# A decoder block in fp32r on one core: the compression's first layer as a stream of its own, a rotary table scaled ahead, more weight tiles, wider splits and another written order

## The chip, the core and the metric

The kernel runs on one core of a Trainium2 chip. A core has five engines with an instruction queue each, worked off in order: TensorE (PE in the profile, PEld for its weight loads), VectorE (DVE), ScalarE (ACT), GpSimd (POOL) and SyncE (SP, which here issues nearly all transfers). They meet at semaphores. The matmuls write to eight PSUM banks of 128 x 512 fp32. The metric is the device time of one execution, in microseconds (us); lower is better.

## The reference

A hybrid decoder block on `x` of 512 tokens by 1024. Cut to what matters:

```python
h = rms_norm(x, norm_pre)
proj = h @ w_in          # split into 15 parts
(q_n, k_c, v_c, k_s, v_s, k_w, v_w, g_n, z_n, q_r, k_r, v_r, z_r, m_a, m_b) = ...
# mixer A: sparse attention, 8 heads of 64, 2 groups
q_n, k_c, k_s, k_w = (apply_rotary(., nsa_ang) for each)
kc = gelu(blocks(k_c) @ cmp_w1_k) @ cmp_w2_k      # compress_blocks: 32 tokens x 64 -> 256 -> 64
vc = gelu(blocks(v_c) @ cmp_w1_v) @ cmp_w2_v
o_a = gated sum of softmax attention over compressed, selected and sliding keys
y_a = (o_a * silu(z_n)) @ w_nsa_o
# mixer B: retention, 4 heads, chunks of 128
q_r = apply_rotary(q_r, ret_ang); k_r = apply_rotary(k_r, ret_ang) * 128 ** -0.5
o_b = retention_sequence(q_r, k_r, v_r)
y_b = (o_b * silu(z_r)) @ w_ret_o
merged = sigmoid(m_a) * y_a + sigmoid(m_b) * y_b
out = x + rms_norm(merged @ w_out, norm_post)
```

Input and output are fp32, and the products are wanted at nearly that precision.

## The kernel before

**Products.** Each fp32 product is three fp32r products: both operands are split into a high part (rounded to fp32r) and a low part (the rest), and high x high, high x low and low x high are summed in PSUM. The transposed input's parts are `hTh` and `hTl`. The weights come as one stream in the order in which they are used. `load_next` issues a transfer of 512 KB on SP into one of four buffers `raw` (L442, L445). `splitter` writes the high half of a raw half-tile into `whi` (ScalarE L224, or VectorE's cast L232), `split_lo` the low half into `wlo` (VectorE's subtraction, L236). A weight tile is one `whi` and one `wlo` of 128 x 512. There are `NW = 9` of them in a ring, and a split waits till the matmuls that read the oldest are through.

**The order is written out.** The kernel is a set of coroutines. `main` goes through the projections and products on TensorE; the others are side work: the tails that read a bank after a block, the attention, the splits. A planner (`Order`) keeps estimated clocks of the engines and asks at each step which coroutine can go on; a table of margins by coroutine (`MARGINS`) and priorities decide among them. What comes out is a fixed sequence for each engine. The hardware only adds the waits.

**The sequence of `main`.** First A (the 512 columns of the sliding and selected keys and values), C (280 columns for the compression and the gates), Q. Then `hidden`, the first layer of the compression, for the keys and then the values: 8 tiles each, 64 matmuls of 256 columns (L272) that read the regrouped tokens `Xs` in `arena_r`. Then the blocks of `PLAN`: Z (the gate of mixer A, 8 tiles with 4 x 3 matmuls of 512 columns each), MA, ZR, QK (queries and keys of the retention), VR (its values), PAIR (QK and ZR of the other two heads), VR of them, MB, NO, RO and so on to the output projection. A block of 128 tokens is 24 matmuls of 512 columns into one bank of the ring `ACC` (banks 84 and 85). Its tail must have read the bank before the next but one block. `hidden` takes one bank of `ACC` for the keys and one for the values. The rings of two banks each besides are `PS` (86, 87) and `PO` (90, 91) for the attention and `PT` (88, 89) for transposes.

**The rotary of the retention.** `tail_qk` runs after each 128-token block of QK, eight times in all: four `scalar_tensor_tensor` of 256 elements that read the bank, multiply by the row's scale `rs` and by a table of sines or cosines (L249), then a subtraction and an addition, then transposes. The table `rtab` has one buffer, loaded again (L1117, on SP) after each step. `ret` is the tail of a value block: high part on ScalarE, low part on VectorE (both scaled by `rs`, into `arena_r`). For the last 128 tokens it first copies the whole bank out and goes on from the copy.

**Sums on POOL.** 25 sums of weights are made in DRAM by transfers that accumulate, issued by `weight_sums`: six after the input's transposed halves are done (flag `hq`), the others after Z's first block.

Of the kernel before, what the change touches and what calls it, by code (L numbers as in the profile page):

```python
# [34 lines left out]
MARGIN = 50  # L35
MARGINS = {'att_cmp': 50.0, 'att_head': 0.0, 'att_out': 1300.0, 'att_sum': 400.0, 'att_unit': 100.0, 'compress': 1300.0, 'ga_split': 1300.0, 'gates': 800.0, 'h_sums': 1000.0, 'keep': 100.0, 'kept': 50.0, 'qk_end': 250.0, 'ret': 20.0, 'ret_state': 0.0, 's_early': 0.0, 's_late': 1000.0, 'seven_end': 0.0, 'split_lo': 20.0, 'splitter': 250.0, 'tail_a': 20.0, 'tail_c': 250.0, 'tail_m': 800.0, 'tail_o': 20.0, 'tail_q': 50.0, 'tail_qk': 600.0, 'tail_yb': 20.0, 'tail_z': 50.0, 'x_split': 0.0, 'zr_end': 1700.0}
SOON = 2
PSOON = 8
# [3 lines left out]
SIGN, SIGN_LAG = 3, 19000.0  # L42
HOLD_C = 300
# [4 lines left out]
DVE_BIAS = 500  # L48


class Order:
# [16 lines left out]
    def spawn(self, gen, prio):  # L68
        self.cos.append([prio, self.n, 0.0, gen])
        self.n += 1  # L70
# [80 lines left out]
def block_kernel(ctx: ExitStack, tc, x, xT, x0s, ws, small, w2s, norm_post, rope_r, dmask, out):  # L151
# [276 lines left out]
    WC = [tuple(at(44, 4480, FR)[:, (2 * p + i) * 280:(2 * p + i + 1) * 280] for i in range(2)) for p in range(KD)]  # L428

    def in_ring(p):  # L430

        return min(p, KD) + max(p - 2 * KD, 0) - sum(min(max(p - 2 * i, 0), 2) for i in sload)
# [24 lines left out]
    def used_up(r):  # L457

        done.append(r)

    nxt = [0]

    def splitter():
        for i, (_, pieces) in enumerate(loads):
            n = sum(pieces)
            for k in range(2):
# [7 lines left out]
                yield lambda: own or in_ring(p) < in_ring(len(done)) + NW  # L474
# [4 lines left out]
                r = max(raws[i][1], done[-1] if done and not own else sfree.get(sload.get(i), 0.0))  # L479
                yield r, "act"  # L480
                m = n // 2
                src = raws[i][0][:, k * m:(k + 1) * m]
                if late >= 0:
                    hi, lo = at(4 * late, 512, FR), at(4 * late + 2, 512, FR)
                elif i in sload:
                    hi, lo = (a[:, k * 512:(k + 1) * 512] for a in SB[sload[i]])
                elif own:
                    hi, lo = WC[p - KD]
                else:
                    hi = wp.tile([P, 512], FR, name="whi", tag="whi", bufs=NW)  # L490
                    lo = wp.tile([P, 512], FR, name="wlo", tag="wlo", bufs=NW)
# [8 lines left out]
                od.spawn(split_lo(p, hi, lo, src, vh, vl, e), rank(p))  # L500
                nxt[0] = p + 1
                yield

    def split_lo(p, hi, lo, src, vh, vl, r):
# [7 lines left out]
        parts.append((hi, lo, r))  # L512
        if p % 2 and len(raws) <= p // 2 + NR:
            load_next()
# [9 lines left out]
    class Block:  # L524


        def __init__(self, nk, n):
            self.base, self.nk, self.n = used[0], nk, n
            used[0] += nk
# [275 lines left out]
    def hidden(i):  # L805

        yield od.need(f"xs{i}")
        yield xr[i] + PE_LAG
        blk = Block(8, 512)
        ph = yield from ACC.get()  # L810
        for c in range(8):
            yield blk.ready(c)
            yield blk.ready(c)
            hi, lo, r = blk.views(c)
            for l in range(2):
                st = Xs[i][:, 2 * c + l].rearrange("p s c -> p (s c)")
                mm(ph[:, 0:256], st, apart(hi[:, l * 256:(l + 1) * 256]), c + l == 0, False, r)
                e = mm(ph[:, 0:256], st, apart(lo[:, l * 256:(l + 1) * 256]), False, c + l == 8)
                yield
            used_up(e)  # L820
        od.spawn(compress(i, ph, e), 1)

    def compress(i, ph, e):
# [4 lines left out]
        e = act(hs, ph[:, 0:256], r=e)  # L828
# [587 lines left out]
    def tail_m(half, i, ps, e):  # L1416
        if half == 0 and i >= 4:
            yield od.need(f"ret0{i - 4}")
# [591 lines left out]
```

## Time and profile before

| | us |
|---|---|
| median of three runs (489.18 to 493.0) | 489.67 |
| the profiled execution | 489.62 |
| its span, first to last instruction | 487.8 |
| TensorE busy | 473.0 (97%) |
| VectorE busy | 422.1 (87%) |
| ScalarE busy | 323.4 (66%) |
| GpSimd busy | 38.9 (8%) |
| DMA, mean over the span | 202 GB/s |

In the lines of the profile, L12 is line 12 of the kernel. A matmul's row has its start, how long it lasted, the tiles it writes and reads, and in brackets how long the engine stood idle ahead of it and what released it. The ends of matmuls are modelled and overlap with the next start, so what a matmul costs is read from start to start.

### The profile page before, as it was taken

The numbers are of one execution on the slowest core, as the hardware profiler recorded it, in microseconds if no ns is written. First come the engines' busy times: TensorE is split into PE (matmuls) and PEld (weight loads), VectorE is DVE, ScalarE is ACT, GpSimd is POOL, SyncE is SP. The second block draws the span as 40 slices with busy tenths as digits, with TensorE's granted clock in tenths as the row PEclk, the third lists the DMA queues.
The fourth block names the chain that finished last, engine by engine and source line by source line (L and its number), as shares of the span: only waits on it lengthen the run. The fifth ranks groups of instructions, "written<-read, shape, count | busy, mean of one in ns | idle before, by whom it ended". The sixth has DMA issues, their size and how long they took to land.

```text
span 487.8 us, 7885 instructions
## 1 busy us (share of the span) xinstructions
PE 473.0 (97%) x2666; PEld 421.2 (86%) x2666; DVE 422.1 (87%) x993; ACT 323.4 (66%) x725; POOL 38.9 (8%) x66
## 2 busy tenths in 40 slices
PE   8999998999999999999999999999999999999993
PEld 7899886889888888887988888998889999988882
DVE  5799899979999999897898999887777868889787
ACT  5796699667789899783686755745435535538542
POOL 3004000112103000000100001010000000000010
PEclk9999999999999999999999999999999999999998
DMA  8989997799987997134678652710574725535914
GB/s 309 394 303 300 321 250 251 190 196 278 318 185 167 345 278 211 59 117 142 134 247 257 225 174 77 204 44 26 164 245 134 254 87 185 188 146 162 310 48 172
DMA packets 31080, 98.75 MB, mean 202 GB/s; under 512 B 3136, under 2 KB 6976, under 8 KB 30272
## 3 DMA queue, kind: packets, MB, share of 16 engines
q1 hardware_dynamic: 24576, 70.85, 43.1%
q0 software_dynamic: 6320, 27.26, 23.2%
q8 instruction: 21, 0.34, 0.3%
q14 instruction: 19, 0.16, 0.1%
q10 hardware_dynamic: 144, 0.14, 0.1%
HBM read 93.52 MB, written 31.98 MB: 257 GB/s over the span
## 4 chain that ended last, share of the span: by engine, by line
PE 82%; ACT 6%; DVE 6%; DMA 3%; issue 2%; SPq 1%; POOLq 0%; POOL 0%; DVEq 0%; ACTq 0%
PE bank L272 70%; PE bank L1251 7%; PE bank L278 4%; ACT whi L224 3%; ACT words L224 2%; DMA raw<-in_stream_dram 2%; DVE wlo L236 2%; DMA words<-in_xT_dram 1%; DVE words L236 1%; DVE words L249 1%; ACT arena_r L224 1%; DVE arena_r L236 1%; ACT rsrow L224 0%; DVE hTl L236 0%; DVE arena_r L249 0%
## 5 line engine op out<-in xcount | busy, mean ns | idle before, releaser
L224 ACT ACTIVATE whi<-raw 128x512 fp32r<-128x512 f32 x176 | 104.6, 623 | 47.7 <-PE bank L272 33.7
L236 DVE TENSOR_TENSOR wlo<-raw,whi 128x512 fp32r<-128x512 f32 x188 | 122.4, 686 | 6.9 <-ACT whi L224 6.5
L272 PE MATMUL bank<-whi,hTh 128*128 128x512 f32 x192 | 72.0, 396 | 3.1 <-DVE arena_r L249 2.2
L272 PE MATMUL bank<-whi,hTl 128*128 128x512 f32 x192 | 68.9, 379 | 0.0
L272 PE MATMUL bank<-wlo,hTh 128*128 128x512 f32 x192 | 68.9, 379 | 0.0
L272 PE MATMUL bank<-arena_r 128*128 128x256 f32 (+2 forms) x328 | 67.5, 328 | 0.0
L224 ACT ACTIVATE arena_r<-bank 128x512 fp32r<-128x512 f32 (+3 forms) x104 | 49.3, 475 | 27.3 <-PE bank L278 26.1
L272 PE MATMUL bank<-arena_r,whi 128*128 128x512 f32 (+1 forms) x208 | 61.5, 371 | 0.0
L236 DVE TENSOR_TENSOR arena_r<-bank,arena_r 128x512 fp32r<-128x512 f32 (+3 forms) x104 | 56.0, 542 | 5.2 <-ACT arena_r L224 4.3
L224 ACT ACTIVATE words<-words,stat 128x384 f32<-128x384 f32 (+3 forms) x112 | 57.2, 542 | 3.2 <-DVE stat L983 2.0
L272 PEld LDWEIGHTS bank<-arena_r 128*128 128x128 f32 x328 | 51.1, 190 | 5.2 <-DVE arena_r L236 0.4
L272 PE MATMUL bank<-hTh,whi 128*128 128x512 f32 (+1 forms) x144 | 51.3, 356 | 0.0
L272 PE MATMUL bank<-hTh,wlo 128*128 128x512 f32 (+1 forms) x144 | 50.2, 348 | 0.3 <-DVE wlo L236 0.3
L272 PE MATMUL bank<-hTl,whi 128*128 128x512 f32 (+1 forms) x144 | 49.9, 347 | 0.0
L272 PEld LDWEIGHTS bank<-whi,hTh 128*128 128x128 f32 x192 | 36.4, 191 | 8.4 <-DVE arena_r L249 2.6
L272 PEld LDWEIGHTS bank<-arena_r,whi 128*128 128x128 f32 x208 | 39.2, 189 | 5.1
L272 PEld LDWEIGHTS bank<-whi,hTl 128*128 128x128 f32 x192 | 36.3, 189 | 5.1
L272 PEld LDWEIGHTS bank<-wlo,hTh 128*128 128x128 f32 x192 | 36.4, 189 | 4.0
L272 PE MATMUL bank<-arena_r,wlo 128*128 128x512 f32 x96 | 36.4, 379 | 0.0
L224 ACT ACTIVATE words<-words 128x512 f32<-128x512 f32 (+3 forms) x47 | 27.4, 583 | 13.5 <-DVE words L236 7.3
L278 PEld LDWEIGHTS bank<-identr,shorts 128*128 128x128 f32 x268 | 30.2, 141 | 6.3 <-ACT words L224 0.5
L278 PE MATMUL bank<-identr,shorts 128*128 128x128 f32 x268 | 31.9, 239 | 0.3 <-DVE words L236 0.3
(182 smaller groups left out, 883.5 us busy)
## 6 DMA issues: line engine op xcount, KB each, us to landing
raw<-in_stream_dram SPq DMA_DIRECT2D x73, 512.0 KB, 4.6
pair<-in_stream_dram POOLq DMA_DIRECT2D x6, 1024.0 KB, 12.1
t<-in_stream_dram POOLq DMA_DIRECT2D x6, 1024.0 KB, 17.4
out<-in_stream_dram POOLq DMA_DIRECT2D x6, 1024.0 KB, 17.0
words<-in_x_dram SPq DMA_DIRECT2D x8, 512.0 KB, 7.9
raw<-s SPq DMA_DIRECT2D x8, 512.0 KB, 4.3
raw<-pair SPq DMA_DIRECT2D x8, 512.0 KB, 4.3
raw<-t SPq DMA_DIRECT2D x8, 512.0 KB, 4.0
```

Of the source, the lines that this page charges most:

```text
L224: S.activation(o, i, func, **kw)
L236: (V if e == "dve" else G).tensor_tensor(o, a, b, op=op)
L249: V.scalar_tensor_tensor(o, a, s, b, op0=op0, op1=op1)
L272: T.matmul(ps, a, b, start=start, stop=stop)
L278: T.transpose(ps, a, idn)
L1251: T.matmul(ps[m], a, apart(b), start=n in first and s + j == 0, stop=n in last and s + j == 5, skip_group_check=True)
```

## The change

It changes these things together:

- `hidden` becomes one coroutine for both halves, started beside Z, and no longer a part of `main`. The weight stream is reordered: Z's weights ahead of the compression's. Both halves share one bank of `PO` (columns 0 to 255 and 256 to 511), taken before Q and given back when the second half is read. The blocks of QK and the tails of MA and MB wait for the flag `hid`.
- The ring of weight tiles becomes a list: nine as before, two more in words 50 to 57 of the shared space for the loads 12 to 19 (Z and the key half of the compression), free after A and the input's halves are done, and four more in the arena for the loads 24 to 31, free once `hidden` is done.
- `rot_table` multiplies the rotary's table by `rs` on ScalarE as soon as it has landed. `tail_qk` then makes two `tensor_tensor` of 512 elements with the table broadcast over the halves, where it made four scaled ones of 256.
- Splits of C's loads, of the loads that the pairs keep and of the last four loads take a whole raw tile at once (1024 or 560 columns).
- `ret` copies out early nowhere (`EARLY_OUT = ()`).
- Other margins, priorities by coroutine (`PRIOS`), other constants of the planner.

The counts of instructions go from 995 to 958 on VectorE and from 652 to 647 on ScalarE. TensorE keeps 2655, SP 170 and POOL 71.

```diff
-MARGIN = 50
-MARGINS = {'att_cmp': 50.0, ...
+MARGIN = 0.0
+MARGINS = {'att_cmp': 0.0, ...
...
+HFIRST, HWANT = 0, 1
+MORE, MORE2 = range(12, 20), range(24, 32)
+EARLY_OUT = ()
...
+    def fits(p):
+        return [(r, i) for r, i in wfree if i < NW or p // 2 in (MORE if i < NW + 2 else MORE2)]
+
+    wtiles.extend((words(50 + 4 * i, 512, FR), words(52 + 4 * i, 512, FR)) for i in range(2))
+    wtiles.extend((at(44 + 4 * i, 512, FR), at(46 + 4 * i, 512, FR)) for i in range(4))
+
+    def more_tiles():
+
+        yield od.need("A0", "A1", "A2", "A3", "hq")
+        wfree.extend((last[1], NW + i) for i in range(2))
+        yield od.need("hid")
+        wfree.extend((hfree[0], NW + 2 + i) for i in range(4))
...
+                wide = i in sload or i >= len(loads) - 4 or KD <= p < 2 * KD
+                if wide and k:
+                    continue
-                yield lambda: own or in_ring(p) < in_ring(len(done)) + NW
+                yield lambda: own or fits(p)
...
-                m = n // 2
+                m = n if wide else n // 2
...
-    def hidden(i):
-
-        yield od.need(f"xs{i}")
-        yield xr[i] + PE_LAG
-        blk = Block(8, 512)
-        ph = yield from ACC.get()
-        for c in range(8):
-            yield blk.ready(c)
-            yield blk.ready(c)
-            hi, lo, r = blk.views(c)
...
+    def hidden(bank):
+
+        for i in range(2):
+            yield od.need(f"xs{i}")
+            yield xr[i] + PE_LAG
+            ph = bank[:, i * 256:(i + 1) * 256]
+            for c in range(8):
+                p = hp[8 * i + c]
+                for _ in range(2):
+                    if HWANT:
+                        wanted[0] = max(wanted[0], p)
+                    yield parts[p][2] + PE_LAG if p < len(parts) else (lambda: p < len(parts))
+                hi, lo, r = parts[p]
+                for l in range(2):
+                    st = Xs[i][:, 2 * c + l].rearrange("p s c -> p (s c)")
+                    mm(ph, st, apart(hi[:, l * 256:(l + 1) * 256]), c + l == 0, False, r)
+                    e = mm(ph, st, apart(lo[:, l * 256:(l + 1) * 256]), False, c + l == 8)
+                    yield
+                used_up(e, p)
+            od.spawn(compress(i, ph, bank, e), 1)
+        hfree[0] = e
+        od.flags.add("hid")
...
+        od.spawn(rot_table(i, od.dma(P * 2048, r)), 1)
+
+    def rot_table(i, e):
+        yield e, "act"
+        rtr[0] = act(rtab, rtab, r=e, scale=rs(i % 4))
+        od.flags.add(f"rt{i}")
...
-        for i in range(2):
-            e = stt(v1[:, :, i, :], pv[:, :, i, :], rs(t), tv[:, 0], OP.mult, OP.mult, e)
-        yield e, "dve"
-        stt(v2[:, :, 0, :], pv[:, :, 1, :], rs(t), tv[:, 1], OP.mult, OP.mult, e)
-        e = stt(v2[:, :, 1, :], pv[:, :, 0, :], rs(t), tv[:, 1], OP.mult, OP.mult, e)
+        e = tt(v1, pv, tv[:, 0].unsqueeze(2).broadcast_to([P, 4, 2, 64]), OP.mult, e)
+        yield e, "dve"
+        e = tt(v2, pv, tv[:, 1].unsqueeze(2).broadcast_to([P, 4, 2, 64]), OP.mult, e)
...
-        if t == NT - 1:
+        if (hp, t) in EARLY_OUT:
...
+        bank = yield from PO.get()
...
-        for i in range(2):
-            yield from hidden(i)
+        od.spawn(hidden(bank), 1)
...
+            if name == "QK":
+                yield od.need("hid")
```

What this does to the order on TensorE is seen first in `hidden`. Before, its matmuls stand in a row, and the value half (bank 85) follows the key half (bank 84):

```order
L272 MATMUL bank0_84<-whi_976,arena_r_83 128x256
L272 MATMUL bank0_84<-wlo_977,arena_r_83 128x256
L272 MATMUL bank0_84<-whi_976,arena_r_83 128x256
L272 MATMUL bank0_84<-wlo_977,arena_r_83 128x256
L272 MATMUL bank1_85<-whi_998,arena_r_83 128x256
L272 MATMUL bank1_85<-wlo_999,arena_r_83 128x256
L272 MATMUL bank1_85<-whi_998,arena_r_83 128x256
L272 MATMUL bank1_85<-wlo_999,arena_r_83 128x256
```

In the changed kernel, at the compression's first tiles, in bank 90; the rows on bank 84 are Z's, those on 86 and 87 the attention's:

```order
L276 MATMUL bank_84<-hTh,whi_167 128x512
L276 MATMUL bank_84<-hTl,whi_167 128x512
L276 MATMUL bank_84<-hTh,wlo_168 128x512
L276 MATMUL bank_90<-whi_173,arena_r 128x256
L276 MATMUL bank_90<-wlo_174,arena_r 128x256
L276 MATMUL bank_90<-whi_173,arena_r 128x256
L276 MATMUL bank_90<-wlo_174,arena_r 128x256
L276 MATMUL bank_90<-whi_175,arena_r 128x256
L276 MATMUL bank_90<-wlo_176,arena_r 128x256
```

One or two tiles of the compression now stand between those of Z.

The second place is the border between VR's first and second block of tokens on TensorE. QK's last block stands in bank 85 ahead of them. Before, bank 84 ends the first block of VR and begins the second, with two matmuls of the attention (bank 91) between:

```order
L272 MATMUL bank_84<-whi,hTh 128x512
L272 MATMUL bank_84<-wlo,hTh 128x512
L272 MATMUL bank_84<-whi,hTl 128x512
L272 MATMUL bank_91<-arena_r 128x512 x2
L272 MATMUL bank_84<-whi,hTh 128x512
L272 MATMUL bank_84<-wlo,hTh 128x512
```

In the changed kernel there:

```order
L276 MATMUL bank_84<-whi_175,hTl 128x512
L276 MATMUL bank_91<-arena_r 128x512 x2
L282 MATMUL bank_88<-identr,shorts_512_1156 128x128
L282 MATMUL bank_88<-identr,shorts_512_1158 128x128
L282 MATMUL bank_88<-identr,shorts_512_1160 128x128
L282 MATMUL bank_88<-identr,shorts_512_1162 128x128
L282 MATMUL bank_89<-identr,shorts_512_1156 128x128
L282 MATMUL bank_89<-identr,shorts_512_1158 128x128
L282 MATMUL bank_89<-identr,shorts_512_1160 128x128
L282 MATMUL bank_89<-identr,shorts_512_1162 128x128
L276 MATMUL bank_85<-whi_173,hTh 128x512
```

Bank 85 follows bank 84, and transposes stand between. At VR's blocks for the other two heads one bank still serves two blocks one after the other in the changed kernel (bank 85 before, bank 84 now).

The third place is ScalarE, at the scaling of the rotary's table (`words_512_136` is `rtab`), a new row among the attention's exponentials and evictions:

```order
L228 ACTIVATE words_256_141<-words_512_127 128x256
L228 ACTIVATE words_512_136<-words_512_136,rs_191 128x512
L228 ACTIVATE arena_r<-bank_88 128x512
L228 ACTIVATE words_512_128<-bank_90 64x512
L228 ACTIVATE arena_r<-bank_89 32x128 x4
```

It stands between two evictions; before, ScalarE had no part in the rotary until its transposes.

More of the change, by code (lines that the diff above doesn't have):

```diff
@@ L427, in block_kernel @@
     raws, parts, done = [], [], []
-    WC = [tuple(at(44, 4480, FR)[:, (2 * p + i) * 280:(2 * p + i + 1) * 280] for i in range(2)) for p in range(KD)]
-    def in_ring(p):
-        return min(p, KD) + max(p - 2 * KD, 0) - sum(min(max(p - 2 * i, 0), 2) for i in sload)
+    WC = [tuple(at(44, 4480, FR)[:, (2 * p + i) * 560:(2 * p + i + 1) * 560] for i in range(2)) for p in range(KD // 2)]
+    wtiles = [tuple(wp.tile([P, 512], FR, name=f"{n}{i}") for n in ("whi", "wlo")) for i in range(NW)]
+    wfree, slot_of = [(0.0, i) for i in range(NW)], {}
+    def fits(p):
[7 more added lines that the diff above has]
+        wfree.extend((hfree[0], NW + 2 + i) for i in range(4))
+    hfree = [0.0]
     hook = {}
@@ L478, in splitter @@
                         load_next()
-                r = max(raws[i][1], done[-1] if done and not own else sfree.get(sload.get(i), 0.0))
+                r = max(raws[i][1], min(fits(p))[0] if not own else sfree.get(sload.get(i), 0.0))
                 yield r, "act"
-                m = n // 2
+                m = n if wide else n // 2
                 src = raws[i][0][:, k * m:(k + 1) * m]
                 if late >= 0:
-                    hi, lo = at(4 * late, 512, FR), at(4 * late + 2, 512, FR)
+                    hi, lo = at(4 * late, 1024, FR), at(4 * late + 4, 1024, FR)
                 elif i in sload:
-                    hi, lo = (a[:, k * 512:(k + 1) * 512] for a in SB[sload[i]])
+                    hi, lo = SB[sload[i]]
                 elif own:
-                    hi, lo = WC[p - KD]
+                    hi, lo = WC[(p - KD) // 2]
                 else:
-                    hi = wp.tile([P, 512], FR, name="whi", tag="whi", bufs=NW)
-                    lo = wp.tile([P, 512], FR, name="wlo", tag="wlo", bufs=NW)
+                    slot = min(fits(p))
+                    wfree.remove(slot)
+                    slot_of[p] = slot[1]
+                    hi, lo = wtiles[slot[1]]
                 vh, vl = hi[:, :m], lo[:, :m]
@@ L511, in split_lo @@
         yield lambda: len(parts) == p
-        parts.append((hi, lo, r))
-        if p % 2 and len(raws) <= p // 2 + NR:
+        m = size(src) // (1 + wide)
+        parts.extend((hi[:, i * m:], lo[:, i * m:], r) for i in range(1 + wide))
+        if (wide or p % 2) and len(raws) <= p // 2 + NR:
             load_next()
@@ L527, in __init__ @@
         def __init__(self, nk, n):
+            if used[0] == 24:
+                used[0] = 24 + 2 * HFIRST
+            elif used[0] == 32 + 2 * HFIRST:
+                used[0] = 48
             self.base, self.nk, self.n = used[0], nk, n
@@ L1930, in stream_shape @@
     yield from [[560]] * 4
-    yield from [[1024]] * (4 + 8)
-    for b in PLAN:
+    yield from [[1024]] * (4 + 8 + 4)
+    for b in PLAN[1:]:
         yield from ["seven"] if b in SEVEN else ["pair"] if b[0] == "PAIR" else [[1024]] * (2 if b[0] == "NO" else 4)
@@ L1965, in stream @@
     out = [first[0][:, 0:512], first[0][:, 512:1024]] + first[1:] + pair(twos(cols(C_C, 280))) + pair(twos(cols(C_Q)))
+    hidden = []
     for n in ("k", "v"):
         w1 = twos(np.asarray(a[f"cmp_w1_{n}"])).reshape(2, 4, 4, 64, 256)
-        out += list(w1.transpose(1, 0, 3, 2, 4).reshape(4, P, 1024))
-    for name, i in PLAN:
+        hidden += list(w1.transpose(1, 0, 3, 2, 4).reshape(4, P, 1024))
+    out += hidden[:HFIRST] + block(*PLAN[0]) + hidden[HFIRST:]
+    for name, i in PLAN[1:]:
         if (name, i) in SEVEN:
```

54 lines of the change are left out of this document (31 added, 23 removed).

## The prediction

> **What bounds the kernel now.** The page first, for its two opening lines.
>
> ```profile
> span 487.8 us, 7885 instructions
> ...
> PE 473.0 (97%) x2666; PEld 421.2 (86%) x2666; DVE 422.1 (87%) x993; ACT 323.4 (66%) x725; POOL 38.9 (8%) x66
> ```
>
> TensorE bounds it: 14.8 us without it are left in 487.8 of span. The profiled execution took 489.62, so 1.8 lies outside the span; the sum below is made against 489.62, which is 0.05 under the median of the three runs (489.67, 489.18 to 493.0), so nothing is corrected for that. One per cent, about what a measurement of this kernel can tell from no change, is 4.9 us: faster means under 484.7, slower over 494.6.
>
> The change leaves TensorE's 2655 matmuls and transposes as they are. Only waits can go, and the view of TensorE's waits says whose they are (us in total, times, longest):
>
> ```profile
> PE bank L272 <- DVE wlo L236: 2.4, 4, 1.4
> PE bank L272 <- DVE arena_r L249: 2.2, 2, 1.2
> ...
> PE bank L272 <- ACT whi L224: 0.6, 1, 0.6
> ```
>
> All of them are short. The low halves of weight tiles (`wlo`, L236) lead, then the retention's values (`arena_r`, L249). The windows show where they fall; each row has the stretch, its length, then each engine's busy time with its instructions, the clock, the DMA share and GB/s.
>
> ```profile
> core 0: us, PE busy (x) PEld busy (x) DVE busy (x) ACT busy (x) POOL busy (x), PEclk, DMA share, GB/s
> ...
> 60.00:80.00 20.00, 17.69 (x109) 15.10 (x109) 19.63 (x44) 19.80 (x42) 0.00 (x0) 1.00 0.89 243
> 80.00:100.00 20.00, 19.65 (x111) 16.44 (x110) 19.64 (x50) 15.42 (x36) 2.35 (x3) 1.00 0.81 214
> 100.00:220.00 120.00, 120.00 (x676) 105.72 (x675) 111.58 (x320) 102.13 (x273) 14.36 (x17) 1.00 0.80 216
> 220.00:240.00 20.00, 18.99 (x104) 16.54 (x103) 15.23 (x34) 10.05 (x20) 1.59 (x2) 1.00 0.47 118
> ```
>
> From 60 to 100 VectorE is busy 39.27 of 40 us, and TensorE stands for 2.66 of it in this count. From 100 to 220 TensorE has no gap at all, with VectorE at 93%. So VectorE sets the pace only where the work around it is badly mixed: in `hidden`, the compression's first layer.
>
> The busy count hides part of the loss, because the modelled ends overlap waits. I therefore count `hidden` by starts. Its groups from 65.24 (its first matmul) to 80.83 (the end of its last), and rows of its timeline:
>
> ```profile
> L272 PE MATMUL bank<-wlo,arena_r 128*128 128x256 f32 x32 | 9.1, 312 | 2.0 <-DVE wlo L236 2.0
> L272 PE MATMUL bank<-whi,arena_r 128*128 128x256 f32 x32 | 8.3, 281 | 0.0
> ...
> L272 PE MATMUL bank<-arena_r 128*128 128x512 f32 x10 | 3.3, 408 | 0.0
> ...
> L278 PE MATMUL bank<-identr,shorts 128*128 128x128 f32 x14 | 1.8, 243 | 0.3 <-DVE words L236 0.3
> ```
>
> ```profile
> 74.88 0.38 PE L272 MATMUL bank<-wlo,arena_r 128*128 128x256 f32 x1 [1.43 <-DVE wlo L236]
> 75.09 0.28 PE L272 MATMUL bank<-whi,arena_r 128*128 128x256 f32 x1
> 75.20 0.28 PE L272 MATMUL bank<-wlo,arena_r 128*128 128x256 f32 x1
> ...
> 75.92 0.51 PE L278 MATMUL bank<-identr,shorts 128*128 128x128 f32 x4
> 76.27 0.34 PE L272 MATMUL bank<-whi,arena_r 128*128 128x256 f32 x1
> ```
>
> An unhindered 256-column matmul starts 0.11 us after its forerunner (75.09 to 75.20), and four transposes take 0.35 (75.92 to 76.27). For 512 columns I take the start-up, which the change also touches:
>
> ```profile
> 8.69 1.03 PE L272 MATMUL bank<-whi,hTl 128*128 128x512 f32 x4
> 9.55 1.03 PE L272 MATMUL bank<-wlo,hTh 128*128 128x512 f32 x4
> ...
> 11.13 1.13 PE L272 MATMUL bank<-whi,hTh 128*128 128x512 f32 x4 [0.55 <-ACT whi L224]
> ```
>
> Four take 0.86, so 0.215 each. `hidden` at that pace is 64 x 0.11 + 10 x 0.215 + 14 x 0.0875 = 7.0 + 2.2 + 1.2 = 10.4 us, against 80.83 - 65.24 = 15.6. So 5.2 us are lost there.
>
> **Part by part.**
>
> *`hidden` beside Z: 5.0 back.* A weight tile is four matmuls in `hidden`, 4 x 0.11 = 0.44 us of TensorE. VectorE's part of a tile:
>
> ```profile
> 77.68 1.89 DVE L236 TENSOR_TENSOR wlo<-raw,whi 128x512 fp32r<-128x512 f32 x3
> ...
> L236 DVE TENSOR_TENSOR wlo<-raw,whi 128x512 fp32r<-128x512 f32 x188 | 122.4, 686 | 6.9 <-ACT whi L224 6.5
> ```
>
> Three in a row need 1.89, the last of them 0.69, so one starts each 0.60: `hidden` eats tiles faster than they are made, whatever else VectorE does. Z takes 12 matmuls of 0.215 = 2.6 us for each of its 8 tiles. Mixed, 24 tiles x 0.60 = 14.4 us of splits stand beside 8 x 2.6 + 7.0 = 27.7 us of matmuls, with two more tiles to stock for Z and the key half. Of the 5.2 I take 5.0 back; the bounds are 0 (the wait moves into Z) and 5.2.
>
> *Start: 0.7 back.* 11.13 - 9.55 - 0.86 = 0.72. ScalarE shows why:
>
> ```profile
> 9.84 0.72 ACT L224 ACTIVATE hTh<-words,words 128x512 fp32r<-128x512 f32 x1 [1.40 <-DMA words<-in_xT_dram]
> 10.46 0.61 ACT L224 ACTIVATE whi<-raw 128x512 fp32r<-128x512 f32 x1
> ```
>
> The split waits behind an activation that waits 1.40 for its own transfer. The new order puts that split first. Bounds 0 and 0.72.
>
> *VR's second block: 1.3 back; the same place for the other two heads: 0.3.* Timelines at the two places:
>
> ```profile
> 222.69 0.72 PE L272 MATMUL bank<-arena_r 128*128 128x512 f32 x2
> ...
> 224.28 0.87 DVE L249 SCALAR_TENSOR_TENSOR words<-bank,rs,words 128x256 f32<-128x256 f32 x2
> ...
> 224.42 0.48 PE L272 MATMUL bank<-whi,hTh 128*128 128x512 f32 x1 [1.01 <-DVE arena_r L249]
> ```
>
> ```profile
> 292.71 0.57 PE L272 MATMUL bank<-arena_r 128*128 128x256 f32 x4
> ...
> 294.44 0.48 PE L272 MATMUL bank<-whi,hTh 128*128 128x512 f32 x1 [1.15 <-DVE arena_r L249]
> ```
>
> Two consecutive blocks share a bank, because the other bank is still read by a late rotary (224.28). 224.42 - 222.69 - 2 x 0.215 = 1.30. In the new order the second block takes the other bank, and the stall goes if that rotary is done within VR's first block, 24 x 0.215 = 5.2 us; the cover is the rotary's shorter chain (below). If it ends as late as before, at 224.28 + 0.87 = 225.15, the stall is 2.0 instead: bounds -0.7 and 1.3. At the other two heads one bank still serves both blocks; four transposes more stand between, 0.35, of which I take 0.3 (bounds 0 and the whole stall, 294.44 - 292.71 - 4 x 0.11 = 1.3).
>
> *The rotary: VectorE gains, ScalarE pays.* Groups of VectorE, one of ScalarE, and how long the rotary table's eight transfers took to land:
>
> ```profile
> L249 DVE SCALAR_TENSOR_TENSOR words<-bank,rs,words 128x256 f32<-128x256 f32 x16 | 6.9, 474 | 0.0
> ...
> L243 DVE TENSOR_SCALAR words<-words,stat 128x512 f32<-128x512 f32 x8 | 3.6, 487 | 0.0
> ...
> L232 DVE CAST whi<-raw 128x512 fp32r<-128x512 f32 x11 | 4.6, 422 | 0.5 <-PE bank L272 0.5
> ```
>
> ```profile
> L224 ACT ACTIVATE words<-words,rs 128x512 f32<-128x512 f32 x2 | 1.4, 714 | 0.3 <-DVE words L236 0.3
> ```
>
> ```profile
> DMA to landing us min/median/max: 2.6/2.7/8.5
> ```
>
> A step was 4 x 0.474 = 1.90 on VectorE; two products of 512, by the split's 0.686, are 1.37: 0.52 less, 2.1 for the four steps before 220. No row has a tensor_tensor with a broadcast table; from 0.474 (half the elements) to 0.75 (the retention's L249 tail) a step saves 0.4 to 0.95. Five softmax scalings of 512 columns go from VectorE to ScalarE: 1.6 less, two of 384 that come (about 0.42 each) taken off. Four more casts there, 4 x 0.422 = 1.7 more. Together VectorE is 2.0 lighter from 60 to 220, which pays nothing by itself where TensorE is full; it is the cover for the first term.
>
> ScalarE gets 0.714 a step, and a wait for the table's transfer (landing after 2.7 at the median, 8.5 at the worst). At three steps this scaling stands some 11 matmuls of 0.215, 2.4 us, behind the issue. Behind it in ScalarE's queue stand exponentials, evictions and the next `whi`, for which TensorE waits. At the median it holds 0.3 us each, and ScalarE is free for 17.9 of 120 us there. Cost 0.3; bounds 0 and 2.
>
> *The first six sums on POOL* come some 20 matmuls, about 4 us, later, and so the raws of `hidden` are fetched beside them. Landing of raws fetched from 40 to 62 us:
>
> ```profile
> DMA to landing us min/median/max: 8.9/9.7/11.8
> ```
>
> The new order leaves about 42 matmuls, 9 us, from issue to split. That is late by 0.7 at the median and 2.8 at the worst, with stocked tiles before it. Cost 0.5; bounds 0 and 2.
>
> *Wide splits.* Fifteen pairs of subtractions become single ones.
>
> ```profile
> L236 DVE TENSOR_TENSOR arena_r<-words,arena_r 128x1024 fp32r<-128x1024 f32 x2 | 2.4, 1220 | 0.0
> ```
>
> Back to back, two of 512 end 0.60 + 0.69 = 1.29 after the start, one of 1024 after 1.22: 0.07 each, 1.0 in all, mostly in the start and the last 180 us where TensorE doesn't wait for it. Taken as 0; bounds -0.5 (the first half of a tile is ready later) and 1.0. [...]
>
> *VectorE's give-back.* If TensorE's 60 to 220 shortens by 5.0, VectorE must do 150.85 - 2.0 = 148.9 us of work in 155 and is idle for 6.1 (4%) where it was idle for 9.15 (6%). It did 98% from 60 to 100, at the cost seen. I take 1.0; bounds 0 and 3.0 (5.0 less the 2.0 removed).
>
> With the other edits I count nothing: the value half of `hidden` enters the key half's bank 1.4 us of other matmuls after it, which covers an eviction of 256 columns; and the dropped early copy of two retention blocks holds a bank longer, with a whole block in the other one.
>
> Sum: 5.0 + 0.7 + 1.3 + 0.3 = 7.3 back, 0.3 + 0.5 + 1.0 = 1.8 given. 489.6 - 5.5 = 484.1.
>
> **Rivals.**
>
> *A. VectorE is the bound from 60 to 220.* Then that stretch shortens only by what leaves VectorE, 2.0, and not by 5.0 + 1.3 - 1.0. For: 98% from 60 to 100. Against: no wait of TensorE in 120 us at 93%. With 0.7, 0.3 and the costs 0.8: 489.6 - 2.2 = 487.4.
>
> *B. The wait stays, in Z.* The change doesn't do what it says: raws land at 11.8 instead of 9 and tiles are stocked too late, so that `hidden` gives 0 to 2 instead of 5. For: ScalarE was 99% busy from 60 to 80, too. Against: the ratio 14.4 to 27.7. 487.1 to 489.1, say 488.1.
>
> *C. Slower: ScalarE stands still for the tables.* If the transfers land like the slowest (8.5), ScalarE is held 8.5 - 2.4 = 6.1 us at each of the seven later steps. TensorE waits once what is ready for it is used up: nine weight tiles last 9 x 3 x 0.215 = 5.8 us, the attention's evictions, which stand in the same queue, less, and I take 4. So about 2 us are lost at each step, 7 x 2 = 14 on top of the forecast less its own 0.3: 497.8. It decides from 0.8 lost at each, a landing of 2.4 + 4 + 0.8 = 7.2 us. For: DMA engines are 80% busy from 100 to 220. Against: the median of eight landings is 2.7.
>
> **Chances.** Forecast 0.56, A 0.20, B 0.14, C 0.10. The forecast's own bounds run from 489.6 - 7.3 - 1.0 = 481.3 (nothing given back, the whole stall at 294 gone) to about 486.5; three quarters of it, 0.42, lie under 484.7, and 0.01 of A. So faster 0.43, within 1% 0.47, slower 0.10. From 481.3 to 488.8 the range leaves out C, a part of B and little below.
>
> **What would show it.** Right: no wait for `wlo` above 0.3 us between 65 and 90, starts at 0.11 and 0.215; no wait of about 1 us at VR's second block, one at the same place of the other two heads; start-up without the 0.55; ScalarE's wait for `words<-in_rope_r_dram` in all under 2 us. A shows as VectorE at 97% or more from 60 to 220 with TensorE's small waits spread over it; B as waits for `wlo` or `whi` in Z; C as long waits of ScalarE for the table and TensorE's behind it. The prediction is wrong if waits arise in the last 180 us, where I count nothing.

## The result, and the profile after

The changed kernel takes 486.32 us at the median of 9 runs (484.29 to 488.01), before 489.57 (9 runs, 489.15 to 493.0). The ratio is 0.992, with a 95% interval of 0.990 to 0.995. That is 3.3 us faster, 0.7%: inside the range, within 1%, and 2.2 us short of the forecast of 484.1. Two more comparisons of the same two kernels gave 0.9945 (0.9927 to 0.9962) and 0.9923 (0.9904 to 0.9942).

The page of the changed kernel, its two opening lines:

```profile
span 485.5 us, 7846 instructions
...
PE 473.0 (97%) x2666; PEld 420.4 (87%) x2666; DVE 417.8 (86%) x956; ACT 327.6 (67%) x720; POOL 40.8 (8%) x66
```

TensorE's busy time is the same, VectorE has 4.3 us less and ScalarE 4.2 more. TensorE's waits (us in total, times, longest):

```profile
PE bank L276 <- DVE wlo L240: 1.2, 1, 1.2
...
PE bank L276 <- DVE arena_r L253: 0.8, 1, 0.8
PE bank L282 <- DVE words L737: 0.5, 1, 0.5
PE bank L276 <- ACT words L228: 0.5, 1, 0.5
PE bank L282 <- DVE arena_r L240: 0.4, 1, 0.4
```

In this execution the four waits for `wlo` (2.4) have become one, the two of the retention's values (2.2) one. But three kinds above 0.3 us are new. The windows say where (columns as in the prediction):

```profile
60.00:80.00 20.00, 19.87 (x111) 17.60 (x110) 18.82 (x47) 16.85 (x36) 2.38 (x2) 1.00 0.98 262
80.00:100.00 20.00, 19.43 (x125) 16.86 (x125) 18.12 (x38) 17.26 (x36) 2.55 (x3) 1.00 0.76 233
100.00:220.00 120.00, 118.76 (x664) 103.46 (x663) 112.63 (x325) 101.89 (x275) 14.34 (x17) 1.00 0.84 225
220.00:240.00 20.00, 19.82 (x107) 16.83 (x106) 16.29 (x35) 13.53 (x29) 1.59 (x2) 1.00 0.38 91
```

From 60 to 100 TensorE has gained 1.96 us of busy time in the same 40. From 100 to 220, where it had no gap, it now has 1.24. That gap is one wait:

```profile
183.81 0.79 PE L282 MATMUL bank<-identr,shorts 128*128 128x128 f32 x8
184.44 0.45 PE L276 MATMUL bank<-whi,hTh 128*128 128x512 f32 x1
186.13 0.48 PE L276 MATMUL bank<-wlo,hTh 128*128 128x512 f32 x1 [1.24 <-DVE wlo L240]
```

and VectorE's queue in front of it, the softmax of the compressed branch, stands between two low halves:

```profile
181.88 1.29 DVE L240 TENSOR_TENSOR wlo<-raw,whi 128x512 fp32r<-128x512 f32 x2
183.09 0.35 DVE L247 TENSOR_SCALAR words<-words,stat 128x256 f32<-128x256 f32 x1
183.47 0.43 DVE L240 TENSOR_TENSOR words<-bank,cmask 128x256 f32<-128x256 f32 x1
183.93 0.42 DVE L240 TENSOR_TENSOR words<-bank,words 128x256 f32<-128x256 f32 x1
184.39 0.42 DVE L980 TENSOR_REDUCE mx<-words 128x8 f32<-128x256 f32 x1
184.85 0.17 DVE L247 TENSOR_SCALAR mx<-mx 128x8 f32<-128x8 f32 x1
185.05 0.42 DVE L240 TENSOR_TENSOR words<-words,mx 128x256 f32<-128x256 f32 x1
185.39 0.68 DVE L240 TENSOR_TENSOR wlo<-raw,whi 128x512 fp32r<-128x512 f32 x1
```

The whole account goes by starts, since the busy count hides part of a loss. For each matmul or transpose I take the time to the next one's start, less the pace (0.216 us for 512 columns and in proportion), and add that up by stretch. Three profiled executions of the changed kernel stand beside the one of before, and two experiments that follow:

```
us lost by starts    before   changed (3 executions)   e_hfirst   e_hidonly
0 to 60               6.0     6.5    6.6    8.0          6.4         6.1
60 to 100             8.0     3.7    4.5    3.1         11.0         1.6
100 to 180            6.5     6.9    6.3    6.3          8.3        13.1
180 to 200            1.1     3.3    3.8    3.8          1.8         1.9
200 to 240            3.2     2.9    3.4    2.4          2.6         3.2
240 to 300            3.0     3.0    3.0    3.0          3.1        11.9
300 to last matmul    4.4     4.3    4.3    4.3          5.7        18.9
after its start       8.5     7.7    7.0    7.0          7.0         8.3
span                487.8   485.5  486.0  485.1        493.1       512.3
```

The pace is too short for transposes (four take 0.35 us, the pace gives them 0.22), so not all of a number is waiting, and what counts is the difference between columns. So `hidden` and Z gave 3.5 to 4.9, the end 0.8 to 1.5. Then 2.2 to 2.7 were lost again at 180 to 200, and 0.5 to 2.0 before 60. The changed kernel's three executions took 487.29, 487.91 and 486.94, the one of before 489.62: their differences, 2.3, 1.7 and 2.7, are smaller than that of the medians.

### The profile page after: what moved, and what is told of

Same layout as the page of the kernel before. It is cut to its first block, busy times and chain, and to the rows that moved or that the text cites. A ratio compares the mean times of both kernels' runs of the same rounds, so it can differ in the third digit from the quotient of the medians.

```text
span 485.5 us, 7846 instructions
## 1 busy us (share of the span) xinstructions
PE 473.0 (97%) x2666; PEld 420.4 (87%) x2666; DVE 417.8 (86%) x956; ACT 327.6 (67%) x720; POOL 40.8 (8%) x66
## 4 chain that ended last, share of the span: by engine, by line
PE 68%; DVE 14%; DMA 9%; ACT 4%; issue 3%; SPq 1%; DVEq 0%; POOLq 0%; POOL 0%; ACTq 0%
PE bank L276 57%; PE bank L1303 8%; DVE words L240 4%; DVE wlo L240 3%; DVE arena_r L240 3%; PE bank L282 3%; DMA raw<-in_stream_dram 3%; DMA words<-in_rope_r_dram 3%; ACT arena_r L228 2%; DMA words<-in_x_dram 2%; ACT words L228 1%; DMA words<-in_xT_dram 1%; DVE words L253 1%; DVE words L1032 1%; DMA raw<-out 1%
## 5 line engine op out<-in xcount | busy, mean ns | idle before, releaser
L228 ACT ACTIVATE whi<-raw 128x512 fp32r<-128x512 f32 x166 | 99.9, 626 | 48.7 <-PE bank L276 36.1
L240 DVE TENSOR_TENSOR wlo<-raw,whi 128x512 fp32r<-128x512 f32 x182 | 119.3, 686 | 7.2 <-ACT whi L228 6.5
L228 ACT ACTIVATE words<-words,stat 128x128 f32<-128x128 f32 (+3 forms) x115 | 59.4, 550 | 1.8 <-DVE stat L1032 1.6
L276 PE MATMUL bank<-hTh,whi 128*128 128x512 f32 (+1 forms) x120 | 41.6, 347 | 0.0
L276 PE MATMUL bank<-hTh,wlo 128*128 128x512 f32 (+1 forms) x120 | 40.9, 340 | 0.0
L276 PE MATMUL bank<-hTl,whi 128*128 128x512 f32 (+1 forms) x120 | 40.8, 340 | 0.0
L240 DVE TENSOR_TENSOR words<-bank,words 128x512 f32<-128x512 f32 (+3 forms) x56 | 33.3, 605 | 4.5 <-ACT words L228 2.4
```

Source lines behind the costliest of these rows:

```text
L228: S.activation(o, i, func, **kw)
L240: (V if e == "dve" else G).tensor_tensor(o, a, b, op=op)
L276: T.matmul(ps, a, b, start=start, stop=stop)
```

## The experiments

The kernels of one set ran on one chip, with the kernel before beside them. Where an experiment keeps the order, the planner books what it booked, and only what is written in the diff comes out otherwise. Where it doesn't, the planner writes a new order, and that turned out to matter more than the edit.

**The changed kernel again** (no edit).

> The changed kernel itself, for a second profile beside the kernels of this call. Median 485.5 to 487. Theory VectorE (the new order puts attention work ahead of a weight tile's low half at 184 us, and that is fixed by the order): the wait of 1.2 us for `wlo` near 184 and those near 28 and 53 us are there again within 0.3 us. Rival (they come from where transfers happened to land in that execution): at least one of the three is gone or over twice as long.

Measured: 487.87 (487.0 to 488.63), ratio 0.9945. The waits are there again: by starts 0.52 near 28, 0.58 near 53 and 1.46 near 185, against 0.63, 0.58 and 1.47. So they look like part of the order; but in the third execution (the base below), where TensorE runs some 1.5 us later after a slow start, the one near 28 is gone, and those at 55 and 185 stay (0.52 and 1.47). What differs besides is the wait near 86 (0.99 against 0.66, none in the third) and the one near 231 (0.80 against 0.33, none in the third).

**The rotary of before, in the order of now.**

```diff
-        rtr[0] = act(rtab, rtab, r=e, scale=rs(i % 4))
+        rtr[0] = od.op("act", act_ns(rtab, rtab, 1), e)   # booked, not issued
-        e = tt(v1, pv, tv[:, 0].unsqueeze(2).broadcast_to([P, 4, 2, 64]), OP.mult, e)
+        for i in range(2):
+            V.scalar_tensor_tensor(v1[:, :, i, :], pv[:, :, i, :], rs(t), tv[:, 0], op0=OP.mult, op1=OP.mult)
+        e = od.op("dve", 1.042 * 512 + 69, e, False)
...
```

> The rotary of before in the order of now: four scaled products of 256 columns where the two of 512 stand, no scaling of the table on ScalarE; every other instruction stays where it is. VectorE gets 8 x 0.5 = 4 us more, 2 of them before 220 us. Theory VectorE is the bound where the new waits are (A): 1.5 to 2.5 slower than the changed kernel, about 488.3. Theory of the forecast (VectorE has cover, and ScalarE's wait for the table costs about 0.3): within 0.5 of it.

Measured: 488.14 (486.18 to 489.79), ratio 0.9951 (0.9934 to 0.9968), beside 0.9945 for the changed kernel: no difference, as the forecast's theory has it. Its groups price the step (count, us in all, mean ns):

```profile
L1184 DVE SCALAR_TENSOR_TENSOR words<-bank,rs,words 128x256 f32<-128x256 f32 x8 | 3.5, 473 | 0.0
L1188 DVE SCALAR_TENSOR_TENSOR words<-bank,rs,words 128x256 f32<-128x256 f32 x8 | 3.5, 474 | 0.0
```

```profile
L240 DVE TENSOR_TENSOR words<-bank,words 128x512 f32<-128x512 f32 x32 | 21.4, 685 | 1.8 <-PE bank L276 1.4
```

The second fence is the changed kernel's; eight of the 8 x 2 products with the broadcast table, those that read a bank, are in that group, at 0.685 like any other. By these means VectorE would be relieved by 8 x (4 x 0.474 - 2 x 0.685) = 4.2 us. But two scaled products in a row overlap and take 0.87, so a step saves 2 x (0.87 - 0.685) = 0.37 and not 0.52: VectorE's busy time is 420.2 with the old rotary, 417.8 with the new one. The time doesn't change, with 2.4 of the 4 us of extra load that the run was meant to have. The first of the eight steps stands at 193 us, so this says nothing on the wait at 184. With the old rotary the waits move: by starts 0.47, 0.40 and 0.44 come at 219 to 223, and the 0.80 near 231 is gone.

**No scaling of the table.**

```diff
-        rtr[0] = act(rtab, rtab, r=e, scale=rs(i % 4))
+        rtr[0] = od.op("act", act_ns(rtab, rtab, 1), e)
```

> The changed kernel without the scaling of the rotary's table on ScalarE (that factor is left out; VectorE reads the table as it lands), all else where it is. ScalarE loses 8 x 0.71 of work and the waits of 5.1 us for the table. Theory of the forecast (the hold costs 0.3): 0 to 0.6 faster than the changed kernel. Rival C in part (ScalarE held by the table is what the chain runs through at 221 to 226 and 57 to 66 us): 1.5 to 3 faster.

Measured: 486.65 (485.46 to 487.84), ratio 0.9923 (0.9903 to 0.9943). The median is 1.2 under the changed kernel's of that set, but the intervals overlap, so neither theory is decided. Its loss from 200 to 240 is 2.3, beside 2.4 to 3.4 for the changed kernel.

**The compression's weights ahead of Z's.**

```diff
-HFIRST, HWANT = 0, 1
+HFIRST, HWANT = 8, 1
```

> The changed kernel with the compression's weights ahead of Z's in the stream, as before: `hidden` stands nearly alone again, all else planned by the same rules. Forecast's theory (5.0 us came from the mixing): 3.5 to 5.5 slower than the changed kernel, 489.8 to 491.8, with waits for `wlo` in `hidden` of over 2 us. Rival (the gain is from the start and the other parts): within 1.5 of it.

Measured: 494.88, ratio 1.0096 (1.0072 to 1.012), 7.0 slower than the changed kernel. The table above has it: 60 to 100 loses 11.0 where the changed kernel loses 3.1 to 4.5, and every other stretch stays within 2.1. So the place is as forecast, and the loss is larger than I expected. The kind of wait is not what I expected either. TensorE's waits, the first three:

```profile
PE bank L282 <- DVE arena_r L240: 2.2, 2, 1.8
PE bank L282 <- ACT arena_r L228: 1.7, 1, 1.7
PE bank L276 <- DVE stat L1032: 1.3, 2, 1.1
```

With `hidden` alone on TensorE, the attention's own steps fall behind on VectorE and ScalarE, not `wlo`. Nor is all of the 11.0 waiting. From 80 to 100 TensorE has no gap, but the granted clock (the third number from the right) is 0.85:

```profile
60.00:80.00 20.00, 15.29 (x97) 12.78 (x95) 18.55 (x48) 16.89 (x37) 2.38 (x2) 0.98 0.99 261
80.00:100.00 20.00, 20.00 (x105) 17.92 (x106) 18.42 (x41) 16.68 (x38) 0.00 (x0) 0.85 0.69 230
```

In windows of 2 us it is 0.50, 0.50 and 0.52 from 80 to 86, behind two waits of 1.66 and 1.78 at 78 and 80.

By starts, the matmuls from 79.9 to 85.8 lose 3.1 us, of which the transposes among them would lose 0.2 at the full clock too. Without the 2.9 some 8.1 is left, as in the kernel before (8.0). The mixing is worth 3.6 to 5.0 by this comparison, and the rest of the 7.0 is the halved clock and what the new order loses elsewhere.

**The first step alone.** The changed kernel with the planner's numbers of before, nine tiles, the rotary of before, narrow splits and the early copies:

```diff
-MARGINS = {'att_cmp': 0.0, 'att_head': 150.0, ...
+MARGINS = {'att_cmp': 50.0, 'att_head': 0.0, ...
-PRIOS = {'att_block': 0, ...
+PRIOS = {}
-MORE, MORE2 = range(12, 20), range(24, 32)
-EARLY_OUT = ()
+MORE, MORE2 = range(0), range(0)
+EARLY_OUT = ((0, 3), (1, 3))
-                wide = i in sload or i >= len(loads) - 4 or KD <= p < 2 * KD
+                wide = False
...
```

> The first step alone: `hidden` beside Z as in the changed kernel, everything else (rotary, narrow splits, nine tiles, early copies, the planner's numbers) as before. Forecast's theory (the mixing gives 5 us by itself, the rest gives some of it back): 484.5 to 487 on a chip where before is 489.6, that is 2.5 to 5 faster than before. Rival (the mixing pays only with the new numbers and more tiles): within 1.5 of before or slower.

Measured: 516.79 (514.09 to 519.55), ratio 1.055: 26 slower. The rival holds (it had "or slower", though not by so much). In its place the step does what it should, and more: from 60 to 100 only 1.6 are lost.

```profile
60.00:80.00 20.00, 20.00 (x110) 17.74 (x109) 19.40 (x45) 17.95 (x37) 2.36 (x3) 1.00 0.79 219
80.00:100.00 20.00, 20.00 (x123) 17.99 (x122) 18.51 (x43) 17.43 (x40) 3.38 (x5) 1.00 1.00 235
```

TensorE has no gap in those 40 us. But 31 us more than before are lost elsewhere, 7 from 100 to 180, 9 from 240 to 300 and 14 or 15 after that. Without the rest of the change the step is worth less than nothing. Two of the other parts are small by themselves (the old rotary above, the narrow splits at the end below), so I take the planner's old numbers to be the reason, which place the rest badly around the new stream. That is argued: no run has the old numbers or the nine weight tiles alone.

**Narrow splits at the end**, order kept: two instructions of 512 columns where one of 1024 stands, for the last four loads.

```diff
-            r = sub_split(vl, src, vh, r)
+            for j in range(2):
+                c = slice(j * m, (j + 1) * m)
+                V.tensor_tensor(vl[:, c], src[:, c], f(vh)[:, c], op=OP.subtract)
+            r = od.op("dve", 1.042 * size(src) + 69, r, near(vl, src, vh))
...
```

> The changed kernel with the last four loads split in halves again, two instructions where one of 1024 stands, everything else where it is. Theory wide splits (the 1.4 us by which VectorE's last operations end earlier after the last matmul come from them): 0.8 to 1.5 slower than the changed kernel, with the span's end 7.8 to 8.5 after the last matmul's start instead of 7.0. Rival (the gain there is from the other order of the tail): within 0.4 of it.

Measured: 486.59, ratio 0.994 (0.9918 to 0.9961), and its span ends 7.2 after the last matmul's start. The rival holds: the wide splits are not what shortened the end.

**A later estimate for the table.**

```diff
-        od.spawn(rot_table(i, od.dma(P * 2048, r)), 1)
+        od.spawn(rot_table(i, od.dma(P * 2048, r) + 2500.0), 1)
```

> The changed kernel with 2.5 us more in the planner's estimate of when the rotary's table has landed, so that ScalarE's scaling stands further behind in its queue; the order on TensorE is the same up to matmul 1129, all else planned by the same rules. Theory (ScalarE held by the table costs 1.2): ScalarE's waits for the table under 1.5 us instead of 5, TensorE's wait near 231 gone, 0.7 to 1.5 faster than the changed kernel. Rival (the rotary then is the late one, and VR's second block waits for it): same or slower.

Measured: 496.27, ratio 1.0123. ScalarE doesn't wait for the table at all any more, and yet the kernel is slower than before, and 9.7 slower than the one with narrow splits at the end, which ran beside it and equals the changed one. The planner wrote a new order from matmul 1129 on, in which 200 to 240 loses 9.2 instead of 2.4 to 3.4. The rival had the sign and part of the reason: the rotary is late, and it is VR's first block that waits for its second product (1.18 us at 218.7). Two waits just ahead of it (0.76 and 0.68) and this one are followed by 5 us at a granted clock of 0.50 (the matmuls at 219.30 and 219.73 start 0.43 apart). What the run tells besides is how much an order depends on one number.

**An earlier eviction of the key half**, by the planner.

```diff
-'compress': 1300.0
+'compress': 0.0
```

> The changed kernel with no margin for the eviction of the compression's halves: on ScalarE it stands two operations (an exponential of 512 and an eviction) earlier, the order on TensorE is the same up to matmul 481. Theory (the value half waits 0.7 to 1.0 for the shared bank): that wait near 86 us is gone, and 0.5 to 1.0 faster than the changed kernel if the rest stays. Rival (the wait passes to the next one, VectorE's): within 0.4 of it.

Measured: 497.57, ratio 1.0164. The same lesson: a new order from matmul 481 on, with 5.7 lost from 180 to 200 and 4.8 from 300 to 320. It decides nothing on the shared bank, so the next three keep the order and move single instructions.

**The changed kernel once more**, as their base.

> The changed kernel once more, as the base of the three that follow on the same chip: 0.993 to 0.995 of before.

Measured: 486.88, ratio 0.9923 (0.9904 to 0.9942), just under what was expected.

**The table's scaling five instructions later in ScalarE's queue.**

```diff
-        rtr[0] = act(rtab, rtab, r=e, scale=rs(i % 4))
+        held.append([5, rs(i % 4)])          # issued after five more of ScalarE, or ahead of its readers
+        rtr[0] = od.op("act", act_ns(rtab, rtab, 1), e)
```

> The changed kernel with the order kept, and only ScalarE's scaling of the rotary's table five instructions later in ScalarE's own queue (or directly ahead of its readers). Theory (the hold on ScalarE costs 1.2 at 221 to 231): 0.7 to 1.3 faster than the base, ScalarE's waits for the table under 1.5 us, TensorE's wait near 231 gone. Rival (what is late there is VectorE's rotary, whatever ScalarE does): within 0.4 of the base.

Measured: 488.02 (485.86 to 489.77), ratio 0.9951 (0.993 to 0.9973): not faster. The median is 1.1 above the base, outside the rival's 0.4 as well, but the intervals overlap. The wait for the table is gone from ScalarE. TensorE has no wait near 231, but the base's profile has none there either, so there was little to win in that execution. TensorE waits elsewhere:

```profile
204.99 0.45 PE L286 MATMUL bank<-arena_r,vcs 96*128 96x512 f32 x1 [0.30 <-DVE arena_r L250]
...
220.19 0.48 PE L286 MATMUL bank<-arena_r 128*128 128x512 f32 x1 [0.24 <-DVE arena_r L250]
```

From 200 to 240 it loses 3.2, as much as the changed kernel. Both new waits are for VectorE. The theory misses; that it is the rotary that is late on VectorE, as the rival has it, these rows don't show, since what they wait for is in `arena_r`.

**And the key half's eviction three instructions earlier.**

```diff
+            if i == 0:
+                S.activation(at(32, 256), ph, AF.Copy)
...
-        e = act(hs, ph, r=e)
+        e = act(hs, ph, r=e) if i else od.op("act", act_ns(hs, ph), e)
```

> As f_later, and the eviction of the compression's key half three instructions earlier in ScalarE's queue; nothing else moves. Theory (the value half waits for the shared bank): the wait of 0.5 to 0.8 us near 86 is gone, 0.5 to 0.9 faster than f_later. Rival (the time is lost again to VectorE's backlog at 184): within 0.3 of f_later.

Measured: 486.54, ratio 0.9926 (0.9908 to 0.9944). The median is 1.5 under the run before it, more than either side expected, but the intervals overlap and the base has 486.88: no difference. And the wait has not gone. ScalarE (above) and TensorE (below) at that place:

```profile
83.16 0.63 ACT L234 ACTIVATE whi<-raw 128x512 fp32r<-128x512 f32 x1 [1.80 <-DMA raw<-in_stream_dram]
...
85.34 0.37 ACT L878 ACTIVATE words<-bank 128x256 f32<-128x256 f32 x1
```

```profile
85.77 0.38 PE L286 MATMUL bank<-whi,arena_r 128*128 128x256 f32 x1 [1.35 <-ACT words L878]
```

The eviction is late because ScalarE, four instructions ahead, waited 1.80 for a raw weight tile. That tile was fetched at 70.7 and landed at 83.0. In the changed kernel's three executions the same split also starts 0.1 us behind its tile's landing (82.1, 83.2 and 83.2). So the wait that looks like one for a shared bank is one for the stream.

**And one low half ahead of the softmax.**

```diff
+                if p == 68:
+                    V.tensor_tensor(vl, src, f(vh), op=OP.subtract)   # right behind its high half
```

> As f_later_evict, and one low half (the one for which TensorE waits 1.2 us at 184) six instructions earlier in VectorE's queue, ahead of the compressed branch's softmax; nothing else moves. Theory (the wait is an error of the order, not a lack of VectorE): the wait goes, 1.0 to 1.5 faster than f_later_evict. Rival A (VectorE is the bound there, and what is put behind is waited for next): within 0.4.

Measured: 487.34, ratio 0.9937 (0.9916 to 0.9959): no gain. The median is 0.8 above the run before it, more than the rival's 0.4, with overlapping intervals. The stalled matmul no longer waits, and the next tile's does:

```profile
185.02 0.45 PE L286 MATMUL bank<-whi,hTh 128*128 128x512 f32 x1
...
185.74 0.38 PE L286 MATMUL bank<-whi,hTh 128*128 128x512 f32 x1
187.51 0.48 PE L286 MATMUL bank<-wlo,hTh 128*128 128x512 f32 x1 [1.40 <-DVE wlo L250]
```

1.40 instead of 1.24, one tile on. That tile's low half still stands behind the same softmax. VectorE has no idle time there, and what is put behind is waited for next, as rival A has it at this place. An order with both low halves ahead of the softmax was not run, so an error of the order is not excluded.

## Why the prediction was right, and where not

The time came within the range, but the sum was too high, and 486.3 lies nearer to rival A's 487.4 than to the forecast of 484.1. By the table, the start and the give-back missed most, VR's second block and `hidden` less; a gain at the end that was not forecast makes up for part of it, and that is luck.

**`hidden` beside Z: 5.0 forecast, 3.5 to 4.9 measured** from 60 to 100. With `hidden` ahead of Z again the stretch loses what it lost before, the halved clock taken off. The mechanism stands; the largest waits left there are the one at the shared bank and small ones for `wlo` (by starts 0.24 to 0.57).

**Start: 0.7 forecast and seen.** The matmuls now follow at pace through that point:

```profile
9.12 1.03 PE L276 MATMUL bank<-wlo,hTh 128*128 128x512 f32 x4
9.99 1.03 PE L276 MATMUL bank<-whi,hTh 128*128 128x512 f32 x4
```

But it isn't kept: the order puts transposes near 28 and 53 that wait for VectorE (0.5 and 0.4 in the waits above). I hadn't looked at what the new numbers do before 60, and the sum has no term for it: 0.5 to 2.0 lost where 0.7 back was forecast, a miss of 1.2 to 2.7. The 2.0 is the execution with the slow start that the last section shows.

**VR's second block: 1.3 forecast, between 0.2 lost and 0.8 back measured** from 200 to 240. The stall at the border is gone, as forecast. In its place stand smaller waits, and ScalarE is held by the table:

```profile
226.07 0.72 ACT L228 ACTIVATE words<-words,rs 128x512 f32<-128x512 f32 x1 [2.02 <-DMA words<-in_rope_r_dram]
```

ScalarE's waits for the table come to 5.1 us in three (5.0 and 3.4 in the other executions), with landings of 2.5, 3.4 and 9.1 (least, median, worst). I had put under 2 us as a sign of being right, so that sign failed. TensorE's price for it is too small to measure, which fits the 0.3: the experiments without the scaling, with the old rotary and with a later scaling lie from 1.2 under to 1.1 over the changed kernel, with overlapping intervals. Rival C needed landings of 7.2 at every step, which didn't come.

**The other two heads: 0.3 forecast, 0.3 measured.** By starts the stall went from 1.32 to 1.02. But the stretch from 240 to 300 loses 3.0 in all four columns, so the 0.3 doesn't show in the sum.

**Give-back of VectorE: 1.0 forecast, 2.2 to 2.7 measured.** This term was mis-sized by 1.2 to 1.7, the largest miss next to the start. The amount of work was about right: in the window from 60 to 220 VectorE is busy 149.6 us where I had 148.9 (the 2.1 for the rotary's four steps were too much, by the 0.37 a step it is 1.5). What I had wrong is that an idle share of 4 to 6% over 160 us says little on a stretch of 10: from 180 to 190 it is busy 9.71 of 10. But the share of these 10 us doesn't tell by itself either, for before it was 9.80 there and TensorE didn't wait. What is new is the softmax ahead of a low half that TensorE needs. That a backlog from the earlier gain comes due there fits this, and is argued; the run that moved one low half only shows that this one move doesn't help.

**Raws beside the sums: 0.5 forecast, 0 to 1.0 measured.** Tiles fetched from 50 to 66 us land after 8.5 at the median and 12.9 at the worst; the one that ScalarE waits for, fetched at 70.5 to 71.7, took 11.5 to 12.6. The wait near 86 comes of it: 0.47, 0.81 and none in the three executions (0.66, 0.99 and none by starts). The shared bank, which I had at nothing, is only where it shows. Whether the sums make the tile late is not shown.

**Not forecast: the end, 0.8 to 1.5 faster.** The last matmul starts 8.5 before the end of the span before, and 7.0 to 7.7 now. VectorE's last addition from a bank shows it (before, then after):

```profile
482.24 0.68 DVE L236 TENSOR_TENSOR words<-bank,words 128x512 f32<-128x512 f32 x1
```

```profile
479.92 0.68 DVE L240 TENSOR_TENSOR words<-bank,words 128x512 f32<-128x512 f32 x1
```

Against the last matmuls at 479.38 and 477.86 that is 2.9 behind and 2.1. The wide splits don't do it. What does, the order of the tail or the earlier raws there, stays open; and there is one profile of before to compare with.

**The rivals.** A's number came nearly true: from 60 to 200 the table has 1.0 to 2.4 less, near A's 2.0 and well under the forecast's 4.0 (5.0 less the give-back). Its sign didn't come: VectorE is busy 93% from 60 to 220 (149.6 of 160), not 97%, and more than half of the 2.2 to 2.7 at 180 to 200 is one wait (1.47 by starts). Nor is VectorE the bound throughout, since the old rotary's 2.4 us more on it, from 193 on, changed nothing. So A was real in one place at the most. B didn't come: the waits for `wlo` from 65 to 90 are small, the longest idle time 0.33 in the third execution, a little over the 0.3 that I had set. What the new order does before 60 beside the first split, and at the end, was left out, and there the two errors (0.5 to 2.0 lost, 0.8 to 1.5 gained) partly cancel.

## What to carry to other kernels

When a stall goes away upstream of an engine that is 94% busy, don't go by its mean: look for the place where it has no room and see what stands in its queue ahead of the operand that is needed next. In an order that a planner writes from estimates, one changed number rewrites everything behind it (some 10 us here, twice, and 26 in a third run that changed more), so a part is tested by moving single instructions with all bookings kept. A wait that is removed by moving one operation has to be looked for one tile further on. And before a loss is put down to waits, read the granted clock behind them.

## What the hardware showed

**Waits can cost twice.** In the kernel with the first step alone, TensorE waited 1.35 us, had five matmuls and waited 3.60 us, and the matmuls behind that start 0.43 apart instead of 0.215:

```profile
247.96 0.79 PE L1305 MATMUL bank<-whi,hTh 128*128 128x512 f32 x1 [3.60 <-DVE arena_r L253]
248.55 0.63 PE L1305 MATMUL bank<-whi,hTl 128*128 128x512 f32 x1
248.98 0.63 PE L1305 MATMUL bank<-wlo,hTh 128*128 128x512 f32 x1
```

```profile
248.00:250.00 2.00, 2.00 (x5) 0.50 0.64 221
250.00:252.00 2.00, 2.00 (x7) 0.50 0.14 45
252.00:254.00 2.00, 2.00 (x14) 0.89 0.00 0
```

In the second fence (stretch, length, TensorE's busy time with its instructions, granted clock, DMA share, GB/s) the clock is 0.50 for 4 us, which adds 10 x 0.215 = 2.1 us. In the kernel with the planner's earlier eviction, a wait of 2.35 at 191 did the same: the clock is 0.59 from 191 to 193 and 0.55 from 193 to 195, so (0.41 + 0.45) x 2 = 1.7 us are lost. Its clock over the span of 499.7 us is 0.985, that of the changed kernel 0.997 over 485.5. By an estimate from these, 7.5 less 1.5, it loses some 6 us more to the clock. The 4.3 besides the 1.7 I put down to its waits of 1.84 at 88 and 1.57 at 303, which is not shown.

With the later estimate for the table the halved clock came behind 0.76, 0.68 and 1.18 within 5 us, and with the compression's weights first behind 1.66 and 1.78. The length of one wait doesn't decide it: behind the 1.18, the last of three, the matmuls start 0.43 apart, and behind a single wait of 1.43 at 74.88 in the kernel before the clock is 1.00 and 256 columns take 0.11. The single waits of 1.24 in the changed kernel (186.13) and of 1.40 with one low half moved (187.51) didn't do it either: the clock from 186 to 188 is 1.00 in the first, and matmuls start 0.22 apart in the second. The halved stretches last 3.4 us with the earlier eviction (191.34 to 194.71), 4 in the fence, 5 with the later estimate and 6 with the compression's weights first. Part of what the re-planned kernels lost is this: over the span the clock is 0.980 with the first step alone, 0.985 with the earlier eviction and 0.989 in the other two.

**The same at the start, in one of three executions.** The base's first matmuls after the warm-up start 0.43 apart for 5 us, those of the first execution 0.215:

```profile
5.04 2.07 PE L276 MATMUL bank<-whi,hTh 128*128 128x512 f32 x4 [0.64 <-ACT hTh L228]
6.91 1.91 PE L276 MATMUL bank<-whi,hTl 128*128 128x512 f32 x4
8.62 1.79 PE L276 MATMUL bank<-wlo,hTh 128*128 128x512 f32 x4
10.25 1.03 PE L276 MATMUL bank<-whi,hTh 128*128 128x512 f32 x4
```

It is one kernel and one order. By 60 us the base has lost 1.5 more than the first execution (8.0 against 6.5), and yet its span is the shortest of the three (485.1 against 485.5 and 486.0): that time came back later. The clock column says 1.00 for that stretch, so it has to be read from the starts.
